# A gradient along rows: another assignment of row pairs to partitions, with the first three tiles laid out plainly

## The chip, the core and the metric

The kernel runs on one core of a Trainium2 chip. The metric is the device time of one execution in microseconds. The kernel before takes 1245.87 us in the median of three runs (1245.39 to 1246.18).

## The reference

```python
def setup_inputs():
    return {"x": np.random.randn(8192, 8192).astype(np.float32)}

def reference(x):
    return np.gradient(x, axis=1)
```

Each row is worked on by itself. An inner element of the result is half the difference of its right and its left neighbour; the first element is x[1] - x[0], and the last is x[8191] - x[8190]. 268.44 MB are read and as many written.

## The kernel before

The 8192 rows are cut into 32 tiles of 256 rows (8 MB). In a tile each of the 128 partitions holds a pair of neighbouring rows, that is 2 x 8192 floats or 64 KB, so one partition's part is one contiguous piece of DRAM. Which pair a partition takes is set by the two `rearrange` calls at L28 and L29, for the input and for the output alike. With Q = 4, partition 4a+q takes the tile's row pair 32q+a, for a from 0 to 31 and q from 0 to 3. Partitions 0 to 3 so take the pairs 0, 32, 64 and 96, partitions 4 to 7 the pairs 1, 33, 65 and 97, and so on. In DRAM, a step in `a` is one pair (64 KB) and a step in `q` is 32 pairs (2 MB). Since the rows are independent, the computation doesn't depend on the order of the pairs, as long as a tile's load and store agree.

There are three slots in SBUF (NB = 3), and tile i uses slot i % 3. The result is written over the input in the same slot, shifted by 64 elements (SH). All work of tile i is:

- `load(i)` (L53): one DMA from SP's queue, 8 MB. From tile 3 on it waits for the store of the tile that had the slot before.
- L75, on POOL: the four end differences of each partition's two rows, into a small tile `ends`.
- L81, on DVE: one custom instruction over 16,382 elements per partition, half the difference of the neighbours. It writes wrong values where the two rows of a pair meet, which the next step covers.
- L92, on DVE or POOL: copies the end differences into their places.
- `store(i)` (L57): one DMA from SP's queue, 8 MB. For the middle tile of each three, L99 and L100 keep the store back until the next tile has landed.

The order of the work is written out by hand: three loads first, then for each tile its compute and its store, and after each third tile the next three loads. All 64 DMAs are issued by SP in this order, to one queue, whose packets are spread over 16 DMA engines. Both DMA lines take their DRAM side from `x_sets[i]` and `out_sets[i]`.

Of the kernel before, what the change touches and what calls it, by code (L numbers as in the profile page):

```python
# [1 line left out]

# [4 lines left out]


@with_exitstack
def kernel(  # L10
    ctx: ExitStack,
    tc: tile.TileContext,
    x: bass.AP,
    out: bass.AP,
):

    nc = tc.nc
    P = nc.NUM_PARTITIONS
    n, m = x.shape
    R = 2  # L20
    NB = 3
    SH = 64
    W = R * m
    nsets = n // (P * R)
    f32 = x.dtype

    Q = 4
    x_sets = x.rearrange("(s q a t) m -> s a q (t m)", q=Q, a=P // Q, t=R)  # L28
    out_sets = out.rearrange("(s q a t) m -> s a q (t m)", q=Q, a=P // Q, t=R)  # L29

    pool = ctx.enter_context(tc.tile_pool(name="pool", bufs=1))
    edge = 256 // 4
    nends = nsets * R * 2
    ends_pad = pool.tile([P, nends + edge // 2], f32, name="ends", tag="ends")
    ends = ends_pad[:, 0:nends].rearrange("p (s t e) -> p s t e", t=R, e=2)
    slots = [pool.tile([P, SH + W], f32, name=f"slot{k}", tag=f"slot{k}") for k in range(NB)]
    loads, stores = [], [None] * nsets
    in_front = {}

    def chain(i, ins, *needed):  # L40

        group, engine = f"slot{i % NB}", ins.ins.engine
        keep = [o.ins for o in needed]
        if in_front.get(engine, (None,))[0] == group:
            keep.append(in_front[engine][1])
        tc.declare_no_dep(ins.ins, group=group, keep=keep, reason="implied by the needed step")
        tc.add_to_no_dep_group(group, ins.ins)
        in_front[engine] = group, ins.ins
        return ins

    def load(i):
        b = slots[i % NB]
        ins = nc.sync.dma_start(out=b[:, SH : SH + W], in_=x_sets[i])  # L53
        loads.append(chain(i, ins, *([stores[i - NB]] if i >= NB else [])))

    def store(i, done, later):
        ins = nc.sync.dma_start(out=out_sets[i], in_=slots[i % NB][:, 0:W])  # L57
        stores[i] = chain(i, ins, done)
        if later is not None:
            tc.add_manual_dep(  # L60
                ins.ins,
                later.ins.name,
                mybir.DependencyInfo(mybir.DependencyClass.Sync, mybir.DependencyReason.DATA),
                reason="issued once the next tile has landed",
            )

    held = None
    with tc.manual_schedule():
        for i in range(NB):
            load(i)  # L70
        for i in range(nsets):
            b = slots[i % NB]
            xin = b[:, SH : SH + W].rearrange("p (t m) -> p t m", m=m)

            ins = nc.gpsimd.tensor_sub(  # L75
                out=ends[:, i, :, :],
                in0=xin[:, :, 1 : m : m - 2],
                in1=xin[:, :, 0 : m - 1 : m - 2],
            )
            at = [chain(i, ins, loads[i])]  # L80
            ins = nc.vector._custom_dve(  # L81
                dve_ops.TENSOR_TENSOR_REDUCE_SUB_MAX,
                out=b[:, 1 : W - 1],
                in0=b[:, SH + 2 : SH + W],
                in1=b[:, SH : SH + W - 2],
                s0=0.0,
                s1=0.5,
            )
            halved = chain(i, ins, *at)
            res = b[:, 0:W].rearrange("p (t m) -> p t m", m=m)  # L90
            placer = nc.gpsimd if i % 5 in (1, 3) and i < nsets - 2 else nc.vector
            ins = placer.tensor_copy(out=res[:, :, 0 : m : m - 1], in_=ends[:, i, :, :])  # L92
            placed = chain(i, ins, halved)
            if held is not None:
                store(*held, at[0])
                held = None
            if i % NB == 1 and i + 1 < nsets:
                held = i, placed
            else:  # L99
                store(i, placed, None)  # L100
            if i % NB == NB - 1:
                for k in range(i + 1, min(i + 1 + NB, nsets)):
                    load(k)


# [1 line left out]
_INS = ['x']  # L107
_OUTS = [((8192, 8192), 'float32')]


# [23 lines left out]
```

## Time and profile before

| | |
|---|---|
| median of three runs | 1245.87 us (1245.39 to 1246.18) |
| the profiled execution | 1246.28 us |
| its span in the profile | 1244.3 us |
| DVE busy | 554.6 us (45%) |
| POOL busy | 8.8 us (1%) |
| DMA packets | 9217, 536.88 MB |
| L81 on DVE | 32 times, 17223 ns each |
| L75 on POOL | 32 times, 198 ns each |
| L92 on POOL and DVE | 12 times 189 ns, 20 times 171 ns |
| a load from issue to landing (median) | 57.9 us |
| a store from issue to landing (median) | 40.2 us |

The span runs from the first instruction to the last. The profile divides it into 40 equal slices and gives, for each, the busy tenths of each engine, the busy share of the 16 DMA engines and the GB/s that they moved. Below that, it lists for each engine what it waited for, in total microseconds, times, and the longest. "SPq" is the queue of SP, the engine that issues the DMAs. Windows give the same busy times and rates for stretches of one's own choice. The trace also has a record of each single DMA packet with its start, its duration and its size; in this kernel a data packet is the 64 KB of one partition, and the 1024 packets of a few bytes are the 16 completion signals of each of the 64 transfers.

### The profile page before, as it was taken

How to read it: one execution, taken by the hardware profiler on the slowest of the kernel's cores; microseconds unless marked ns; L12 is line 12 of the kernel's file. 1: busy time of each engine (PE TensorE's matmuls, PEld its weight loads, DVE VectorE, ACT ScalarE, POOL GpSimd, SP SyncE). 2: the span in 40 equal slices, each digit the busy share in tenths (PEclk: the TensorE clock that was granted, in tenths of full speed). 3: DMA queues.
4: the chain of work that ended last, by engine and by line, in shares of the span. 5: the costliest groups of instructions: out<-in, count | busy, mean ns of one | idle time of the engine just before them, and what ended most of it. 6: DMA issues, size and time to landing. Idle time of an engine off the chain costs nothing.

```text
span 1244.3 us, 237 instructions
## 1 busy us (share of the span) xinstructions
DVE 554.6 (45%) x52; POOL 8.8 (1%) x48
## 2 busy tenths in 40 slices
DVE  2850483069009702850582079009603840591082
POOL 0000000000000000000000000000000000000000
DMA  9999999999999999999999999999999999999999
GB/s 404 432 421 428 436 438 438 438 436 436 428 423 434 438 438 436 436 438 432 426 428 438 438 436 436 438 438 426 423 436 438 434 438 438 438 430 426 430 407 404
DMA packets 9217, 536.88 MB, mean 431 GB/s; under 512 B 1024, under 2 KB 1024, under 8 KB 1024
## 3 DMA queue, kind: packets, MB, share of 16 engines
q1 hardware_dynamic: 9216, 536.88, 99.7%
q14 instruction: 1, 0.01, 0.0%
HBM read 268.44 MB, written 268.44 MB: 431 GB/s over the span
## 4 chain that ended last, share of the span: by engine, by line
another core or an unknown queue 74%; DVE 18%; DMA 3%; issue 2%; POOL 1%; SPq 0%; POOLq 0%
DVE slot L81 18%; DMA slot<-in_x_dram 3%; POOL ends L75 0%; POOL slot L92 0%; SPq L53 0%; POOLq L129 0%; DVE slot L92 0%
## 5 line engine op out<-in xcount | busy, mean ns | idle before, releaser
L81 DVE CUSTOM_DVE_ANT_0 slot<-slot 128x16382 f32<-128x16382 f32 x32 | 551.1, 17223 | 667.1 <-POOL ends L75 667.1
L75 POOL TENSOR_TENSOR ends<-slot 128x4 f32<-128x4 f32 x32 | 6.3, 198 | 988.0 <-DMA slot<-in_x_dram 988.0
L92 POOL COPY slot<-ends 128x4 f32<-128x4 f32 x12 | 2.3, 189 | 207.8 <-DVE slot L81 207.8
L92 DVE COPY slot<-ends 128x4 f32<-128x4 f32 x20 | 3.4, 171 | 0.7
L118 POOL MEMSET const-bfloat16-1.0<- 128x1 bf16 x1 | 0.1, 101 | 0.0
L118 POOL MEMSET const-uint8-127<- 128x1 uint8 x1 | 0.1, 101 | 0.0
L118 POOL MEMSET const-float32-0.0<- 128x1 f32 x1 | 0.1, 98 | 0.2 <-issue 0.2
L118 POOL MEMSET const-float32-1.0<- 128x1 f32 x1 | 0.1, 98 | 0.0
## 6 DMA issues: line engine op xcount, KB each, us to landing
slot<-in_x_dram SPq DMA_DIRECT2D x32, 57.9
out_dram<-slot SPq DMA_DIRECT2D x32, 40.2
```

Of the source, the lines that this page charges most:

```text
L75: ins = nc.gpsimd.tensor_sub(out=ends[:, i, :, :], in0=xin[:, :, 1 : m : m - 2], in1=xin[:, :, 0 : m - 1 : m - 2],)
L81: ins = nc.vector._custom_dve(dve_ops.TENSOR_TENSOR_REDUCE_SUB_MAX, out=b[:, 1 : W - 1], in0=b[:, SH + 2 : SH + W], in1=b[:, SH : SH + W - 2],
L92: ins = placer.tensor_copy(out=res[:, :, 0 : m : m - 1], in_=ends[:, i, :, :])
L118: nc = _bacc.Bacc("TRN2", target_bir_lowering=False, num_devices=1)
```

## The change

The factor Q goes from 4 to 8, and the first three tiles no longer use it. In tiles 0, 1 and 2 partition p takes row pair p (plain). In the other 29 tiles partition 8a+q takes row pair 16q+a, for a from 0 to 15 and q from 0 to 7: partitions 0 to 7 take the pairs 0, 16, 32 up to 112, partitions 8 to 15 the pairs 1, 17, 33 up to 113. A step in `a` is one pair (64 KB), a step in `q` is 16 pairs (1 MB). Input and output are laid out in the same way. The DRAM side of the DMAs so has the shape [128, 16384] for the first three tiles and [16, 8, 16384] for the others, where it was [32, 4, 16384] for all. Everything else is as before.

```diff
-    Q = 4
-    x_sets = x.rearrange("(s q a t) m -> s a q (t m)", q=Q, a=P // Q, t=R)
-    out_sets = out.rearrange("(s q a t) m -> s a q (t m)", q=Q, a=P // Q, t=R)
+    Q = 8
+
+    def sets(t):
+
+        plain = t.rearrange("(s p t) m -> s p (t m)", p=P, t=R)
+        dealt = t.rearrange("(s q a t) m -> s a q (t m)", q=Q, a=P // Q, t=R)
+        return [plain[i] if i < NB else dealt[i] for i in range(nsets)]
+
+    x_sets, out_sets = sets(x), sets(out)
```

## The prediction

> **What bounds the kernel now.** I read the page's header and parts 1 to 3 first, then SP's waits, the loads by their line, the windows by stage, and last the trace's records of the single DMA packets.
>
> ```profile
> span 1244.3 us, 237 instructions
> DVE 554.6 (45%) x52; POOL 8.8 (1%) x48
> DMA  9999999999999999999999999999999999999999
> GB/s 404 432 421 428 436 438 438 438 436 436 428 423 434 438 438 436 436 438 432 426 428 438 438 436 436 438 438 426 423 436 438 434 438 438 438 430 426 430 407 404
> q1 hardware_dynamic: 9216, 536.88, 99.7%
> ```
>
> No engine but the DMA engines is near full: DVE works 45% of the span, the one DMA queue has packets on its 16 engines for 99.7% of it, and all 40 slices show the 9. The rate is flat but for the first slice and the last two.
>
> ```profile
> SPq L57 <- DVE slot L92: 508.0, 20, 55.7
> SPq L53 <- DMA out_dram<-slot: 365.7, 29, 18.7
> ...
> POOL ends L75 <- DMA slot<-in_x_dram: 988.0, 32, 77.7
> ...
> DMA to landing us min/median/max: 22.8/57.9/61.4
> ```
>
> These lines are two of SP's waits (us in total, times, longest), the longest of the engines' waits, and the loads of L53 from issue to landing. The engines wait for data (988.0 us), and SP waits for engines and for stores, but its waits leave no hole: a load is issued a median of 57.9 us before it lands, three times the 19.3 us that one transfer takes (below). So there is nearly always a transfer queued behind the running one.
>
> ```profile
> 2.20:60.90 58.70, 34.62 (x3) 0.58 (x3) 1.00 1.01 425
> 60.90:120.00 59.10, 17.39 (x2) 0.20 (x1) 1.00 1.00 435
> 120.00:1120.00 1000.00, 462.00 (x42) 7.43 (x38) 1.00 1.00 434
> 1120.00:1204.00 84.00, 23.16 (x4) 0.20 (x1) 1.00 0.96 415
> 1204.00:1244.30 40.30, 17.39 (x2) 0.20 (x1) 1.00 0.96 416
> ```
>
> The columns are the stretch, its length, busy DVE and POOL with their instructions, clock, DMA share and GB/s. From 60.9 to 1120 us the DMA share is 1.00 at 434 to 435 GB/s. Only the beginning and the end are lower.
>
> The packets say how this rate is made. There are 64 transfers of 128 packets of 64 KB, 8 packets for each of 16 engines. Of 8192 packets all but 77 take between 2415 and 2440 ns, and the median is 2418 ns: 65,536 B / 2418 ns = 27.1 GB/s, times 16 = 434 GB/s, the rate of the window. Eight in a row give a cadence of 19.32 us per transfer, measured between the mean packet starts of following transfers. So the time is made of:
>
> - 2.2 us from the span's start to the first packet;
> - 64 x 19.32 = 1236.5 us of packets at their common pace;
> - 0.77 us (mean over the engines) because the first 16 packets, those of the very first load, take 2.4 to 3.6 us;
> - 0.90 us because all 16 first packets of the very first store, at 58.4 us, take 2.9 to 3.8 us;
> - 0.40 us from all other longer packets together (the excess over 2418 ns of all packets, divided by 16, is 2.07 us; less 0.77 and 0.90);
> - about 2.1 us near 1204 us, where the loads have run out and the last but one store waits for DVE (the cadence there is 21.48 us in place of 19.32), and some 0.3 us of small gaps;
> - 1.1 us from the last packet's end, at 1243.2 us, to the span's end.
>
> This is 1244.3 us. The profiled execution took 1246.28 us, 2.0 us more than its span, and lies 0.4 us above the median of the three runs, 1245.87 us. What can be told from no change here is about 0.2%, 2.5 us.
>
> **The change part by part.** Both programs have the same instructions in the same order on each engine: 66 on SP, 54 on DVE, 53 on POOL, with the same waits. A partition still takes two whole rows, so L75, L81 and L92 work on tiles of the same shape and none of their durations (198, 17223, 171 to 189 ns) has a cause to change. Nothing is added, removed or moved on any queue. What changes is the DRAM address of each packet, and the shape in which SP's DMA instruction states the DRAM side: [128] in place of [32,4] for three tiles (6 transfers), [16,8] in place of [32,4] for 29 tiles (58 transfers). Packets stay 64 KB, and the records should still hold 9216.
>
> *The plain tiles.* Six transfers, 6 x 19.32 = 116 us. Their packets may gain at most what exceeds the pace: 0.77 + 0.90 = 1.7 us, if the two slow beginnings come from the dealt addresses. They may lose at most, if every packet were like the slow beginnings (3.25 us mean, 0.83 above the pace), 48 x 0.83 = 40 us. I take 0. Row pairs were dealt in the same way at every later load and store, and the other beginnings of transfers have no such row of 16 slow packets: at 120 us three packets are long, at 175 us seven. So the two slow beginnings look like a first use of the input and of the output, and stay with any layout; and after the first packet the pace is 2418 ns whatever address follows.
>
> *The tiles dealt by 8.* 58 transfers. They can gain what is left of the 0.40 us, as no packet is shorter than 2415 ns. For the loss the nearest row is again the slow beginning: if the new addresses made the first packet of each engine collide in each transfer, 58 x 0.83 = 48 us. I take 0, since between 0 and 0.83 us per transfer the row it is nearest to is the dealing by 4, where engines read pairs 64 KB apart for over a thousand microseconds at one pace. Within a partition group the step falls from 32 pairs (2 MB) to 16 pairs (1 MB), the step between groups stays one pair.
>
> [...]
>
> *Who is behind.* Were a transfer later by some microseconds, the next ones in the queue would be later by the same, since the queue is never empty; DVE has 17.4 us of work against 38.6 us of transfers per tile and would only wait longer. So each microsecond lost on packets is one on the end. A gain would also pass through, up to the 17.4 us of DVE before the last two stores, which stay.
>
> **Sum.** 1246.28 + 0 (plain) + 0 (dealt by 8) = 1246.28 us for a profiled execution; beside the median of the runs, 1245.9 us. Bounds: -1.7 - 0.4 = -2.1 us (1243.8 beside the median), and above +40 + 48 us (1334); a price for every packet of the dealt tiles is a rival.
>
> **The rivals.**
>
> *Faster by more than 2.5 us.* All that the addresses could give back is 2.1 us. It would need packets shorter than the 2415 ns that 8192 of them never go below. Chance 0.03, time about 1243.
>
> *The first packets collide (slower).* With eight pairs per group and 16 groups, all engines start a transfer on 16 neighbouring pairs, in one megabyte, and the two slow beginnings show that packets can cost 0.83 us more when all engines start together. For it: in both, all 16 engines are hit. Against it: no later transfer shows it, and there engines start their packets up to 2.4 us apart, a whole packet. It decides if the engines fall into step at each transfer; it begins to count from three such beginnings (2.5 us) and its full price is 58 x 0.83 = 48 us, so 1294. The plain tiles being slower belongs here, as the price is on the same packets. Chance 0.17, with most of it below 1290.
>
> *Addresses alias throughout (slower).* If not the first but every packet of the 58 transfers took what a packet of the slow beginnings takes, 58 x 8 x 0.83 = 385 us, so 1631. For it: engines 64 KB apart are sixteen in a row now. Against it: in the slow beginnings themselves the second packet of each engine is back at 2418 to 2420 ns, 64 KB apart as before. Chance 0.04. [...]
>
> *The engines' shares change (slower).* SP's DMA instruction has to cut 128 partitions and the DRAM shape into 16 shares that fit each other. With [32,4] a share could be two blocks of four partitions from different places; with [16,8] one block of eight is the only cut along the first dimension. If two engines then need the same path into SBUF at the same time, each packet takes up to twice 2418 ns, on 58 transfers: 58 x 19.32 = 1121 us more, 2367 us. It would decide from the first dealt tile on, at 120 us. For it: the outer dimension is now exactly the number of engines. Against it: the trace shows 16 equal engines and nothing of ports, so there is no row in which two of them share. Chance 0.15.
> [...]
>
> *The change doesn't do what it says.* If the lowered DMAs had other packets than 64 KB, the counts would tell. The program's shapes show [128], [16,8] and 16,384 elements as said; 0.01.
>
> **How the numbers follow.** No change 0.60, colliding beginnings 0.17, aliasing throughout 0.04, shares 0.15, faster 0.03, other 0.01 (counted as slower). So faster 0.03, same 0.60, slower 0.37. The forecast is the likeliest case, 1245.9 us. Its own range is 1243.4 to 1248.4. The range of 8 in 10 adds the faster case's edge and nearly all of the colliding beginnings, and leaves out aliasing throughout and the shares, which lie far off with 0.19 together: 1243.4 to 1290.
>
> **What would show it.** Right: packets at 2418 ns, a cadence of 19.32 us per transfer from tile 3 on, 434 GB/s in the window from 120 to 1120 us, and the same two slow beginnings. Layout at fault in the beginnings: packets of 2418 ns at 2.2 and 58.4 us. Collisions: 16 long packets at the head of each transfer, and the digits of GB/s lower throughout. Shares: packets of up to 4.8 us from the fourth load on, while the first three loads keep 2418 ns. The forecast is wrong if any stage after 120 us is below 430 GB/s.

## The result and the profile after

The changed kernel takes 2230.41 us (median of six runs, 2199.34 to 2235.40), the kernel before 1245.74 us beside it (six runs, 1245.19 to 1246.18). The medians differ by 984.7 us. The ratio of the fast runs is 1.7817 (95% interval 1.7754 to 1.7881); it leaves out the slowest two of the six, the profiled one among them, which lie 1.5 and 1.6% above the fastest and count as slow. The forecast of no change was wrong, and the range up to 1290 us too; the rival of the engines' shares had given 2367 us.

The profiled execution took 2235.4 us, with a span of 2233.5 us. These are the lines of its page that answer to those of before:

```profile
span 2233.5 us, 237 instructions
DVE 554.6 (25%) x52; POOL 8.9 (0%) x48
DMA  9999999999999999999999999999999999999998
GB/s 425 420 244 207 232 228 216 212 252 266 217 214 255 243 212 215 259 254 209 236 229 242 210 236 259 239 211 242 237 231 208 247 249 228 210 250 248 218 214 191
q1 hardware_dynamic: 9216, 536.88, 98.9%
```

The DMA engines look nearly as busy as before (98.9% beside 99.7%), and the packets have the same number and the same bytes. Only the rate differs, and it breaks in the third slice. "Busy" says that packets are under way, not that they move at full speed. By stage (stretch, length, busy DVE and POOL, clock, DMA share, GB/s):

```profile
2.20:60.90 58.70, 34.62 (x3) 0.59 (x3) 1.00 0.98 413
60.90:120.00 59.10, 17.40 (x2) 0.20 (x1) 1.00 1.05 441
120.00:600.00 480.00, 103.85 (x9) 1.77 (x9) 1.00 1.00 226
600.00:1120.00 520.00, 138.64 (x13) 2.17 (x11) 1.00 0.99 232
```

Up to 120 us, where only plain tiles move, the rates are close to those of before (425 and 435 GB/s). With the first dealt tile the rate falls to about half and stays there. The waits grow with it (engine, line, whom it waited for: total us, times, longest), while DVE's work of 554.6 us is as before:

```profile
POOL ends L81 <- DMA slot<-in_x_dram: 1950.1, 32, 151.6
SPq L63 <- DVE slot L98: 788.3, 20, 90.8
SPq L59 <- DMA out_dram<-slot: 738.8, 29, 38.1
```

The packet records say the same closer up. In the plain tiles the median packet takes 2418 ns; from 125 to 240 us the mean is 5080 ns, 2.10 times as much. Later the packets of the dealt tiles spread between 2418 and 5900 ns; their mean over all is 4.502 us. That gives 58 x 8 x (4.502 - 2.418) = 967 us, nearly all of the loss. The engines have packets under way nearly all the time; the packets are slow, and from 125 to 240 us none took less than 4.9 us.

### The profile page after: what moved, and what is told of

Same layout as the page of the kernel before. It is cut to its first block, busy times and chain, and to the rows that moved or that the text cites. A ratio compares the mean times of both kernels' runs of the same rounds, so it can differ in the third digit from the quotient of the medians.

```text
span 2233.5 us, 237 instructions
## 1 busy us (share of the span) xinstructions
DVE 554.6 (25%) x52; POOL 8.9 (0%) x48
## 2 busy tenths in 40 slices
DMA packets 9217, 536.88 MB, mean 240 GB/s; under 512 B 1024, under 2 KB 1024, under 8 KB 1024
## 3 DMA queue, kind: packets, MB, share of 16 engines
q1 hardware_dynamic: 9216, 536.88, 98.9%
## 4 chain that ended last, share of the span: by engine, by line
another core or an unknown queue 84%; DVE 10%; DMA 2%; issue 2%; POOL 0%; SPq 0%; POOLq 0%
DVE slot L87 10%; DMA slot<-in_x_dram 2%; POOL ends L81 0%; POOL slot L98 0%; SPq L59 0%; POOLq L135 0%; DVE slot L98 0%
```

## The experiments

Two theories were left. **Shares**: the DRAM shape [16,8] makes each DMA engine carry eight neighbouring partitions, and pairs of engines then need one path into or out of SBUF. **Addresses**: the order of the row pairs makes packets collide in DRAM. The kernel before took 1246.0 to 1246.3 us (medians) beside these runs. The records of packets don't name their engine, so the numbers of engines below are names that the theory gives, and who shares with whom is read from durations.

### The same neighbourhoods of DRAM, stated as [16,8] and as [32,4]

Tiles are taken two by two, and of their 256 row pairs partition 8a+q, or 4a+q, takes one near its neighbour's. The lines for the input, in short:

```diff
-    x_sets = x.rearrange("(s q a t) m -> s a q (t m)", q=Q, a=P // Q, t=R)
+    two = x.rearrange("(g a s q t) m -> g s a q (t m)", a=P // Q, s=2, q=Q, t=R)
+    x_sets = [two[i // 2, i % 2] for i in range(nsets)]
```

The output goes the same way, and Q is 8 in one run, 4 in the other.

> All tiles. Two tiles share 256 neighbouring row pairs, and partition 8a+q takes pair 16a+8s+q of them (s = 0 or 1): DRAM shape [16,8], but each partition group of eight lies in one piece of DRAM, and the groups are 1 MB apart. Shares theory (a first dimension of 16 makes each engine carry eight neighbouring partitions, and pairs of engines then need the same path into SBUF): packets of 4.8 to 5.1 us and about 2250 to 2400 us, as no tile is plain. Addresses theory (the order of pairs 16q+a makes packets collide in DRAM): the order is gone, so 1246 us and packets of 2418 ns. Theory that the change's plain tiles are at fault for what follows: 1246 us as well, since there are none.

> The twin of the run with [16,8]: partition 4a+q takes pair 8a+4s+q of the same 256 pairs, DRAM shape [32,4]. A partition's piece of DRAM lies at most 512 KB from where it lies in the twin. Shares theory: 1246 us, packets of 2418 ns, cadence 19.32 us, because the first dimension is 32 again. Addresses theory: the same time as the twin, whatever that is.

Measured: 2317.98 us with [16,8] (one run), and 1246.59 us with [32,4] (1246.31 to 1247.62; ratio to before 1.0003, 0.9994 to 1.0012). The windows of the [16,8] run, and below them those of the [32,4] run:

```profile
2.20:60.90 58.70, 16.23 (x1) 0.20 (x1) 1.00 1.03 214
60.90:120.00 59.10, 18.39 (x3) 0.39 (x2) 1.00 1.03 213
120.00:1120.00 1000.00, 225.28 (x21) 3.55 (x18) 1.00 0.99 235
```

```profile
2.20:60.90 58.70, 34.62 (x3) 0.59 (x3) 1.00 1.00 423
60.90:120.00 59.10, 17.39 (x2) 0.20 (x1) 1.00 1.01 437
120.00:1120.00 1000.00, 460.67 (x42) 7.49 (x38) 1.00 1.00 433
```

About the same DMA share stands beside 213 to 235 GB/s in one and 423 to 437 in the other. The order of pairs 16q+a is in neither, so it isn't the cause; the shape [16,8] is enough to bring the loss, from the first load on.

### The plain tiles alone

```diff
+        return [plain[i] if i < NB else dealt[i] for i in range(nsets)]
```

with Q = 4 in the dealt tiles.

> The plain tiles alone: tiles 0 to 2 plain, the others dealt by 4 as before. Both theories: 1245.7 us within 2.5 us. What it decides is whether the plain layout takes away the slow first packets (0.77 us at the first load, 0.90 us at the first store): by the prediction they stay, and the time is the same within 0.1%; if they came from the dealt addresses, 1.7 us (0.13%) less.

Measured: 1245.99 us (1245.44 to 1246.59; ratio 0.9998, 0.9989 to 1.0007). The first packets of the first load exceed 2418 ns by 0.60 us in the mean (0.77 before), and the first 16 of the first store take 3.4 to 3.9 us (2.9 to 3.8 before). The slow beginnings stay with the plain layout, as the prediction had it, and this half of the change costs and gains nothing that can be told.

### Longer and shorter first dimensions

Only Q is changed in the kernel before, to 2 ([64,2]) and to 16 ([8,16]).

> All tiles dealt by 2: DRAM shape [64,2], partition 2a+q takes pair 64q+a, 4 MB between neighbours of a partition pair. Shares theory: 64 divides into blocks of four partitions as 32 x 4 does, so 1246 us and 2418 ns. Addresses theory: with the longest step of all it should be as slow as the step of 1 MB or slower.

> All tiles dealt by 16: DRAM shape [8,16]. Shares theory: the first dimension of 8 leaves 8 engines, each with 16 neighbouring partitions and 16 packets per transfer; four groups of four partitions per engine, in which engines e and e+2 meet: 16 x 4.84 = 77 us per transfer, 64 of them, so about 4950 us with packets of 4.8 us. If only the number of engines counts: 16 x 2.418 x 64 = 2476 us, so about 2490, with packets of 2.418 us. Addresses theory: no number follows for the packets, but 16 engines stay busy.

Measured: 1246.40 us for [64,2] (1246.05 to 1246.97; ratio 1.0004, 0.9994 to 1.0013), with 4 MB from one partition to the next: a long step by itself costs nothing here. For [8,16] 3687.01 us, between the two numbers. Its page:

```profile
DMA  5455454444544445434454444454445444544443
GB/s 105 105 114 120 127 117 125 166 191 182 168 171 164 132 151 158 160 110 142 153 166 133 153 151 145 132 149 144 155 141 150 153 128 144 142 146 188 204 154 87
DMA packets 8705, 536.88 MB, mean 146 GB/s; under 512 B 512, under 2 KB 512, under 8 KB 512
```

512 completion signals where the other kernels have 1024 are eight for each transfer: half of the engines work, and the DMA share is some five tenths. The first three loads land at 83, 163 and 242 us, 80 us each. Eight engines that share paths in pairs had been expected to take 77, and eight that share nothing 16 x 2.418 = 38.7. Later the rate rises, so the total is far under the 4950 us of the theory. By then the engines have fallen out of step: the eight shares of a transfer land within 1 us of each other up to 242 us, and within 13 us by 451 us.

### Making the engines miss each other

By the shares theory e and e+4 share one path for four packets of a transfer and another path for the next four, and stop hurting each other once one lags by half a transfer. So the changed kernel was given small loads ahead of everything, meant to let one engine of each pair lag: engines 0 to 3 behind 4 to 7, and 8 to 11 behind 12 to 15. Its addresses and shapes are otherwise untouched. The first form put them all into a few partitions:

```diff
+        for first, few in ((0, 4), (16, 12)):
+            ins = nc.sync.dma_start(out=slots[NB - 1][first : first + few, SH : SH + W], in_=x_sets[0][0:few])
```

> The changed kernel with two small loads ahead of everything, one of 4 and one of 12 partitions, into partitions that tile 2's load overwrites later. [...] Shares theory: four packets into one group of four partitions take 4 x 2.4 = 9.7 us each, which is half of one transfer; from then on the engines e and e+4 are never at the same group of partitions, the dealt tiles run at 2418 ns a packet, and the time falls from 2230 to about 1265 us (20 us for the small loads), or to at most 1500 if the lag of 19 us makes SP's queue run dry. Addresses theory: about 2250 us, as no address of the 64 transfers changes; small packets of 2.4 to 3.6 us.

Measured: 2249.30 us (2238.74 to 2250.93), no help. Which engines the small loads run on no record shows; they have 16 completion signals together (1040 packets under 512 B in this run, 1024 in the kernel before), as 4 and 12 engines would give. The small loads took 8 to 11 us a packet, but all 16 engines were slowed by as much meanwhile, those that already worked on the first tile too. So the lag didn't arise: the 16 shares of the first tile's load landed in three groups only 2 us apart (38.4 to 38.6, 40.1 to 40.6, 42.4 to 42.5 us), less than one packet. This run says nothing of the theories; that it meets the 2250 us of the addresses theory is no sign for it, since nothing was shifted. The second form is meant to give four packets to each engine that it uses, in other partitions, and the third is its control:

```diff
+        for first, k in ((0, 4), (40, 12)):        # the control: ((0, 8),)
+            some = x[0 : 4 * k * R].rearrange("(q a t) m -> a q (t m)", q=4, a=k, t=R)
+            ins = nc.sync.dma_start(out=slots[NB - 1][first : first + 4 * k, SH : SH + W], in_=some)
```

> The changed kernel with two other small loads ahead of everything, now into partitions of different groups of four: one of 16 partitions, four packets on each of engines 0 to 3, and one of 48 partitions, four packets on each of engines 0 to 11. Engines 0 to 3 should then lag 4 to 7, and 8 to 11 lag 12 to 15, by four packets, half of a transfer's eight. Shares theory (engine e has partitions 8e to 8e+7 in a dealt tile, and e and e+4 work on the same path for four packets and on another for the next four): with half a transfer between them they never meet, most packets take 2418 ns and the time falls to about 1270 us, or to about 1500 if the lag is worn off in part. Addresses or the cutting of the shape as such: about 2250 us as in the run with the crowded small loads. The small loads' packets: about 2.4 to 3.6 us, where the crowded ones took 8 to 11.

> The control: one small load of 32 partitions, four packets on each of engines 0 to 7, so that 0 to 7 lag 8 to 15 by half a transfer, but e and e+4 do not lag each other. Shares theory with pairs e and e+4: no help, 2200 to 2260 us. If the pairs were e and e+8: about 1270 us here, and 2250 in the other. Addresses: 2250 us.

Measured: 2113.51 us with the lag between e and e+4 (2108.10 to 2119.51; ratio to before 1.695, 1.692 to 1.698), and 2236.61 us in the control (one run). The total hides what happened; the stages show it. With the lag:

```profile
120.00:180.00 60.00, 0.00 (x0) 0.00 (x0) 1.00 1.01 365
180.00:240.00 60.00, 34.62 (x3) 0.59 (x3) 1.00 1.01 325
240.00:300.00 60.00, 17.40 (x2) 0.20 (x1) 1.00 1.00 389
300.00:400.00 100.00, 51.84 (x4) 0.97 (x5) 1.00 0.99 374
500.00:600.00 100.00, 52.00 (x5) 0.59 (x3) 1.00 0.84 202
```

In the control, the same stretches:

```profile
120.00:180.00 60.00, 8.38 (x1) 0.20 (x1) 1.00 1.00 227
180.00:240.00 60.00, 26.24 (x3) 0.39 (x2) 1.00 1.02 210
240.00:300.00 60.00, 17.39 (x2) 0.20 (x1) 1.00 1.02 240
300.00:400.00 100.00, 0.00 (x0) 0.00 (x0) 1.00 0.99 223
```

From 125 to 400 us, 59% of the packets take at most 2440 ns with the lag, 4% in the control, and 3% in the changed kernel as it is. The lags were there: the first tile's load landed at 43.9 to 44.1, 51.8 to 52.1 and 60.2 to 60.4 us, in three groups 8 us apart, as engines with none, four and eight packets ahead would. So the same DMAs run at up to 389 GB/s when the engines' times are shifted against each other in one way, and at 210 to 240 when in another. That is against addresses and against a cost of the shape as such, and for paths that engines share for a part of each transfer. The forecast of 1270 us was too good, and that of 1500 too: the lag doesn't last. From 413 us on one half of a transfer's shares goes on landing at the full cadence (413, 432, 452 us), the other half falls back by 12 to 17 us with each transfer, and by 500 us the early engines wait for the next transfer (DMA share 0.84) and the lags are gone. The small loads' packets missed their forecast as well: 2.7 to 3.4 us at first, then about 5.1 us on all engines until some 36 us (211 GB/s from 5 to 36 us), though by the theory few of them should have met. In the control, where by the theory none met, 88% of the first 256 packets took at most 2440 ns, the longest 3.1 us, and the first 41 us ran at 409 GB/s. So a small load by itself costs nothing, and engines that share a path seem to slow all 16, also those that should have had a path to themselves; the crowded loads, with 103 GB/s over the first 21 us, did the same. How is open.

### Which direction pays

Load and store were dealt by 8 one at a time, in all 32 tiles, the other side plain. Load and store then no longer agree, so the output has the row pairs of each tile in another order than the reference.

> Loads alone dealt by 8, stores plain (the row pairs of a tile are so stored in another order than the reference's). Which direction pays: if loads and stores both pay in the changed kernel, a load takes 38 to 40 us and a store 19.3, together 32 x 58.5 = 1870 us; if only the way into SBUF is shared, about 2200 us; if only the way out, about 1250.

> The counterpart: stores alone dealt by 8, loads plain (again the row pairs are stored in another order). If both directions pay: about 1870 us. If only the way into SBUF is shared: about 1250; if only the way out: about 2200. Either way the sum of what this run and its counterpart add to 1246 us should be what the change adds with all tiles dealt by 8, some 1050 us.

Measured, one run each: 1911.59 us with dealt loads and 1745.06 us with dealt stores. Both directions pay: 665 and 499 us more than 1246.3 us, 1164 together, beside 1072 with both in the [16,8] run above. The forecasts, 1870 us for each and some 1050 us together, came out 2% too low for the loads, 7% too high for the stores and 10% too low for the sum. Dealt loads keep a cadence of 40.3 us for about the first half of the run; dealt stores begin at 36 to 38 us, fall to 29 to 32 within four rounds, and lie mostly between 31 and 39 later.

### The shares written out by hand

Each plain load is cut into eight DMAs of 16 partitions; the stores stay whole. The 256 load DMAs and 32 stores have 4608 completion signals, 16 for each, so a load DMA has one packet on each engine. In one run DMA j takes every eighth partition, in the other 16 neighbours:

```diff
+        for j in range(8):
+            rows = slice(j, 121 + j, 8)            # the other run: slice(16 * j, 16 * j + 16)
+            ins = nc.sync.dma_start(out=b[rows, SH : SH + W], in_=x_sets[i][rows])
```

> The shares written out by hand on plain addresses: each load is cut into 8 DMAs of 16 partitions, DMA j taking partitions j, 8+j, 16+j up to 120+j, one packet on each engine; stores plain and whole. Engines then read at steps of 512 KB. Shares theory: engine e writes partition 8e+j in DMA j, as in a dealt tile, so load packets of 4.8 to 5.1 us, stores 2418 ns. Addresses theory: plain addresses ran at full rate in the changed kernel's first tiles, so 2418 ns for both. The time is also set by a shorter queue (8 DMAs at most are under way), so the packets decide and not the total.

> [...] Shares theory with groups of four partitions: four engines write to one group at a time, so load packets of 4 x 2418 = 9.7 us and loads of 77 us; some 32 x (77 + 19) = 3080 us. [...]

Measured, one run each: 1912.33 us with steps of 8, 0.04% from the 1911.59 us of dealt loads, and 2845.83 us with 16 neighbours. First the step of 8, in a stretch of loads and in one of stores, then the same of the 16 neighbours:

```profile
20.00:120.00 100.00, 34.62 (x3) 0.59 (x3) 1.00 1.02 210
130.00:180.00 50.00, 12.91 (x2) 0.00 (x0) 1.00 1.02 440
```

```profile
20.00:220.00 200.00, 34.62 (x3) 0.58 (x3) 1.00 1.01 112
230.00:280.00 50.00, 15.88 (x2) 0.00 (x0) 1.00 0.99 431
```

The load packets take 5.1 us in the first and 9.37 us in the second, the stores 2418 ns in both. A load DMA lands 40.4 and 72.5 us after its issue in the median, about eight times its packet, as if eight were under way. The total with 16 neighbours is 8% under the 3080 us of its forecast. The 16 neighbours are one megabyte of DRAM in one piece and are the slowest of all, so the loss of the loads goes by partitions and not by addresses. If four partitions in a row have one path, as the theory takes it, sixteen in a row put four engines on each of four paths, and a packet should take 4 times its 2418 ns; measured are 9.37 / 2.418 = 3.9. Sixteen partitions at steps of 8 are in 16 such groups of four and are still slowed by 2.1, as if two groups share one path. By the theory the engines read 512 KB apart here, as they do in the [32,4] twin above, which lost nothing.

## Why the prediction was wrong

**What held.** The bound (the packets' pace), the plain tiles at nothing, the slow beginnings that stay, the unchanged instructions on DVE and POOL, and that each microsecond lost on packets is nearly one on the end: 967 us of longer packets make nearly all of the 989 us between the two profiled executions.

**The step that failed** is the second of the parts, "The tiles dealt by 8": "I take 0, since between 0 and 0.83 us per transfer the row it is nearest to is the dealing by 4". The nearness was judged by addresses. In these runs the first dimension counts: [128], [64,2] and [32,4] run at 2418 ns a packet, [16,8] at 5080 ns as long as the engines are in step, and [8,16] on eight engines at 5.0 us up to 240 us. The price of the step was 58 x 8 x 2.084 us = 967 us, where the prediction had 0. The bound of 48 us for that part had the same fault: it was taken from addresses, and the other way to read the change stood only among the rivals.

**The rival that came true** was "The engines' shares change", with 0.15. It named a cause that the runs agree with (one block of eight partitions as the only cut along a first dimension of 16), the place (120 us) and the sign in the packets ("packets of up to 4.8 us from the fourth load on"). Its price of 1121 us was 14% too high, and two things work against each other in it: from 125 to 240 us a packet takes 2.10 and not 2 times its 2418 ns, but the engines drift out of step from about 300 us on, and 9% of the packets between 1000 and 2000 us then take at most 2440 ns; 4.50 us is the mean over the dealt tiles. What spoke against it, that "there is no row in which two of them share", was no evidence: a kernel whose shares never meet can't show it.

Beforehand, no row showed which partitions an engine gets or which engines would meet: one path for two engines was a guess, and twice 2418 ns an estimate from the packets of before. The shares themselves show in the completion signals, 16 for each transfer with [32,4] and with [16,8] (1024 in all), 8 with [8,16] (512). The runs agree with engines that meet: 2.1 times the 2418 ns for steps of 8, 3.9 times for 16 neighbours, and pairs, e and e+4 by the theory's names, that are helped by a lag between them (325 to 389 GB/s from 120 to 400 us) and not by one between e and e+8 (210 to 240). The prediction had the two blocks of four only as something that "could be", and so gave the rival 0.15 without working out which engines would meet.

**The other rivals.** Colliding first packets: no; from 125 to 240 us every packet is slow, in the middle of transfers as much as at their heads. Aliasing throughout: no; steps of 2 and 4 MB between partitions, and of 512 KB between groups of four, run at 433 to 434 GB/s with a first dimension of 32 or 64. A step of 1 MB between partitions was not run with such a first dimension, but loads from plain addresses are slowed as much without it (5.1 us a packet with steps of 8).

**Open.** The records give no engine, so the assignment itself wasn't seen, only its consequences. The theory of pairs doesn't say why the small loads of two runs slowed engines that should not have met any other, so the picture of separate paths is not complete. Why half of the engines lose their lag after 400 us is open too. The runs with [16,8] in all tiles, with [8,16] and with one direction, the control of the lag and the two with hand-made shares were timed once each; their effects, of 40% and more, are far outside the 1.6% by which the changed kernel's times vary, but the small differences between them are not to be leaned on.

## What to carry to other kernels

In these runs the shape in which a DMA states its DRAM side decided the rate, it seems by deciding which partitions each engine gets. So an access pattern that "only" permutes rows can halve the rate (434 to 226 GB/s here): before changing one, compare its first dimension with that of a pattern known to run at full rate. A DMA share of 0.99 doesn't say that the DMAs run well: it stood beside 232 GB/s, where 1.00 had stood beside 434. The GB/s, or the time of one packet, says it. When a change has two readings, here an order of addresses and a form of instruction, the price of each has to be bounded, and a trace in which a contention never arises is no evidence that it can't.

## What the runs showed of the hardware

- A 64 KB packet took 2418 ns with first dimensions of 128, 64 and 32, 5.1 us in loads of 16 partitions at steps of 8, and 9.37 us in loads of 16 neighbours; the shares theory reads this as one, two and four engines on one path. In the runs with small loads ahead, where by the theory only some engines should have shared, all 16 were slowed, to 5.1 us and to 8 to 11 us.
- The loss is in both directions: some 40.3 us per dealt load, and 36 to 38 us per dealt store at first, in place of 19.3 us.
- In the slow transfers the engines drift out of step by themselves: in the changed kernel the 16 shares of a transfer land within 1.0 us of each other at 160 us, within 3.2 us at 312 us and within 12 us at 382 us. Its rate goes from 199 to 205 GB/s right after 120 us to between 208 and 266 in the slices from 223 to 2178 us, and its times vary by 1.6% from run to run, where the kernel before varies by less than 0.1%.
- Starting some engines half a transfer later gave 325 to 389 GB/s for 280 us with the same DMAs that otherwise moved 199 to 241 GB/s.
